# Weight sums in DRAM stored as whole rows of the weights instead of column blocks

## The chip, the cores and the metric

The kernel runs on one core of a Trainium2 chip. The metric is the device time of one execution in microseconds, the median of several runs. The core has TensorE (PE, with its weight loads shown apart as PEld), VectorE (DVE), ScalarE (ACT), GpSimd (POOL) and SyncE (SP). Transfers are issued from SP's queue, from POOL's and a few from ACT's; all of them are moved by the core's 16 DMA engines.

## The reference

One inference step of a two-layer decoder trunk for 1024 prompt tokens and 64 sample tokens, in float32. Layer 0 mixes with a recurrence (12 heads, with low-rank gates) and a memory attention; layer 1 with latent attention. Behind each mixer stands the feed-forward that this change concerns:

```python
def conv_glu(xn, conv_prev, w_up, conv_w, conv_b, w_down):
    T = xn.shape[1]
    u = xn @ w_up                                  # w_up: 1024 x 5632
    gate, val = u[..., :D_FF], u[..., D_FF:]       # D_FF = 2816
    ext = jnp.concatenate([conv_prev.astype(gate.dtype), gate], axis=1)
    conv = conv_b
    for j in range(CONV_W):
        conv = conv + ext[:, j:j + T] * conv_w[j]
    h = jax.nn.silu(conv) * val
    return h @ w_down, ext[:, T:]
```

## The kernel before

The product with `w_up` is computed in seven block products instead of eight, in the manner of Strassen and Winograd. For that, sums of quarters of the weight are needed. The weight of a layer has four quarters of 512 rows and 2816 columns: gate columns and value columns, each with upper and lower rows. `sum_weights` forms four sums per layer in DRAM, by transfers alone: `vg` (upper value plus upper gate), `gg` (upper gate plus lower gate), `vgg` (`vg` plus lower gate) and `all` (`vgg` plus lower value). A sum starts as a copy, made by SP's queue (L1298 from the weights, L1307 from another sum), and is then added to by adding transfers of POOL's queue (L1303, `accum_op=ALU.add`), each of which reads a piece of the weight and the sum and writes the sum. A sum lies in DRAM as 22 blocks of 128 columns, `[22, 128, 4, 128]`: block, row in its group of 128, group, column. A block that the feed-forward loads is thus one contiguous piece, with 2048 bytes for each of 128 partitions.

The feed-forward (`ffn`, `up`) goes through 22 chunks of 128 columns for each of two halves of the tokens. For a chunk `load_up` (L1325) loads seven blocks of 256 KB on SP's queue: three straight from the weight, four from the sums. ACT and DVE split each into a high and a low part (L1327, L1328), and PE multiplies.

The sums are made long before they are read, while the mixer of layer 0 runs (`mixer_a`). The mixer has 12 units: two halves of the tokens by six pairs of heads. In each step `i` of its loop the front of unit `i` (projections with `w_in_a`, loaded at L207, with the low part of the weights made by POOL at L211), the inner part of unit `i-1` and the recurrence of unit `i-2` are woven together, and beside them up to five steps of `sums`, a step being one transfer. The first step of the loop holds the projections of the memory keys and values instead (`memory_kv`, loads at L2188 of `w_mem_kv`). A scheduler then orders the instructions of every engine; each engine and each queue works its list in that order. A transfer that POOL issues stands in POOL's list among the arithmetic, and what is behind it waits.

Lines that are named below: L614 and L615 clear a part of a small weight tile on POOL, L648 is a product with it on PE; L760 masks a tile on POOL, L766 and L913 are copies on ACT behind it, and L909, L917, L924 the chained products of the recurrence on PE; L1060 stores a unit's output.

Of the kernel before, what the change touches and what calls it, by code (L numbers as in the profile page):

```python
# [14 lines left out]
ALU = mybir.AluOpType  # L15
# [9 lines left out]
DFF = 2816  # L25
# [75 lines left out]
class Step:  # L101
# [171 lines left out]
    def mixer_a(s, od, qmd, kvd):  # L273
        nc, tc = s.nc, s.tc
# [50 lines left out]
        def front(u):  # L325
            h, p = u
            if p == 0:
                yield from s.a_norm(h)
                yield from s.a_lora(h)
            if p == 2:  # L330
                yield from s.a_gate(h)
            ctx[u] = {}
            yield from s.a_front(p, h, ctx[u])

        def chain(u):
            h, p = u
            ctx[u]["y"] = s.t(ap, [128, 576], "y", 2)
            for g in s.groups(h):
                yield from s.a_chain(p, h, ctx[u], *g)
            yield from s.a_out(p, h, ctx.pop(u))  # L340
# [29 lines left out]
        sums = s.seq(s.sum_weights(0), s.sum_weights(1))  # L370
        for i in range(nu):
            g = []
            if i == 1:
                for j in range(1, (len(s.prows) + 127) // 128):
                    s.load_params(j, [nc.sync])
            if i > 1:
                g.append((chain(units[i - 2]), s.PW[0] + s.PW[1] * units[i - 2][0], s.PW[2]))
            if i:
                u = units[i - 1]
                g.append((s.a_inner(u[1], u[0], ctx[u]), s.PW[3] + s.PW[4] * u[0], s.PW[5]))  # L380
            g.append((front(units[i]), 130 if units[i][1] else 220))
            if i == 0:
                g.append((mkv, 22))
            else:
                g.append((s.take(sums, 5), 5))
            s.merge(g)
        s.mslot = (ap, "xn", 584, 16)
        s.drain(last(s.seq(s.mem_attention(0, qmd, kvd, od, ("mm", "sm", "sm")), s.memory_kv(kvd, 1, ("sm", "mm", "mm")))))
# [895 lines left out]
    def sum_weights(s, l):  # L1284

        nc, W = s.nc, s.I["w_ffn_up"][l]
        NCH = DFF // 128
        s.wsum[l] = {z: s.t(s.dp, [NCH, 128, 4, 128], f"ws{l}{z}", 1) for z in ("vg", "gg", "vgg", "all")}
        S = s.wsum[l]

        def quarter(f0, k0):
            for k in range(4):
                r = 512 * k0 + 128 * k
                yield k, W[r:r + 128, f0:f0 + DFF].rearrange("p (c f) -> p c f", f=128)

        def put(z, f0, k0):
            for k, w in quarter(f0, k0):
                nc.sync.dma_start(out=S[z][:, :, k].rearrange("c p f -> p c f"), in_=w)  # L1298
                yield

        def add(z, f0, k0):
            for k, w in quarter(f0, k0):
                nc.gpsimd.dma_start(out=S[z][:, :, k].rearrange("c p f -> p c f"), in_=w, accum_op=ALU.add)  # L1303
                yield

        def copy(z, y):
            nc.sync.dma_start(out=S[z].rearrange("c p k f -> p c (k f)"), in_=S[y].rearrange("c p k f -> p c (k f)"))  # L1307
            yield

        yield from s.seq(put("vg", DFF, 0), put("gg", 0, 0), add("vg", 0, 0), add("gg", 0, 1), copy("vgg", "vg"),  # L1310
                         add("vgg", 0, 1), copy("all", "vgg"), add("all", DFF, 1))

    def load_up(s, l, c, first=False):


        nc, W = s.nc, s.I["w_ffn_up"][l]

        def quarter(f0, k0):
            return W[512 * k0:512 * k0 + 512, f0:f0 + 128].rearrange("(k p) f -> p k f", p=128)

        fv, fg = DFF + 128 * c, 128 * c
        S = s.wsum[l]
        for i, src in enumerate((quarter(fv, 0), S["vgg"][c], S["gg"][c], S["vg"][c], quarter(fg, 1), S["all"][c], quarter(fv, 1))):
            w = s.t(s.wp, [128, 4, 128], "wr", 3) if first and i < 3 else s.st([128, 4, 128], "wa", s.WA)
            nc.sync.dma_start(out=w, in_=src)  # L1325
            wh, wl = (s.t(s.up, [128, 4, 128], z, 5, F32R) for z in ("uh", "ul"))
            nc.scalar.copy(wh, w)  # L1327
            nc.vector.tensor_tensor(wl, w, wh.bitcast(F32), ALU.subtract)  # L1328
            yield [(wh[:, k], wl[:, k]) for k in range(4)]

    def ffn(s, l, xs0, after, pre=None):
# [3 lines left out]
        Wd = I["w_ffn_down"][l]  # L1335
        NCH = DFF // 128
        s.lay(([128, 4, 128], "wa", s.WA))

        cprev = s.st([128, NCH, 16], "cprev", 1)
        cout = s.st([128, NCH, 18], "cout", 1)  # L1340
        cs = I["state_conv"][l].rearrange("b j f -> (b j) f")
        q = s.pst("dn")
        for i in range(0, NCH, 4):
            m = min(4, NCH - i)
            stg = s.st([128, 4, 128], "wa", s.WA).rearrange("p a b -> p (a b)")
# [1091 lines left out]
```

## Time and profile before

| | |
|---|---|
| median of 3 runs | 3641.74 us (3635.59 to 3645.61) |
| the profiled execution | 3667.54 us, span 3665.8 us |
| PE, PEld busy | 91%, 78% of the span |
| DVE, ACT, POOL busy | 64%, 47%, 23% |
| mean granted TensorE clock | 0.929 |
| DRAM read, written | 436.67 MB, 118.03 MB |

The page divides the span into 40 slices and shows for each how busy the engines and the DMA engines were and which clock TensorE was granted. "issue" as what ended an idle time means that the engine waited for nothing that the profile shows. Instructions that issue transfers are not counted as busy time of POOL.

### The profile page before, as it was taken

What the parts mean: (1) busy time and instruction counts of PE and PEld (TensorE: products, weight loads), DVE (VectorE), ACT (ScalarE), POOL (GpSimd) and SP (SyncE); (2) the same over time, 40 slices, a digit from 0 to 9 for tenths busy, and PEclk for the clock granted to TensorE, in tenths of its full rate; (3) what the DMA queues carried; (4) which work ended last, traced back from release to release, by engine and by line L of the source; (5) the groups of instructions that cost most, each with busy time, mean ns of one, the idle gap of its engine ahead of it and who ended that gap; (6) DMA issues with size and microseconds to landing.
All of it is one profiled execution on the core that took longest, in us unless ns stands there. A gap on an engine that the chain in (4) does not pass through costs nothing. (4 is left out here: it accounts for less than half of the span.)

```text
span 3665.8 us, 68595 instructions
## 1 busy us (share of the span) xinstructions
PE 3352.4 (91%) x25782; PEld 2855.6 (78%) x25782; DVE 2331.4 (64%) x5353; ACT 1725.2 (47%) x3769; POOL 851.5 (23%) x1204
## 2 busy tenths in 40 slices
PE   6677689999986999999999999989999999999998
PEld 4444457767754899998999888855558999989998
DVE  4454356767654477778777647743444777787776
ACT  4333245544444564455444635533335644455444
POOL 4343332322101231113212500101112311132221
PEclk9876578988898899999999999999999999999999
DMA  8999991111223354455444311235433454445443
GB/s 198 239 218 221 209 203 34 39 42 40 68 60 128 95 158 136 138 147 154 142 133 140 103 53 30 81 118 171 148 112 108 140 147 133 137 134 148 138 137 114
DMA packets 608368, 466.90 MB, mean 127 GB/s; under 512 B 51354, under 2 KB 530350, under 8 KB 603940
## 3 DMA queue, kind: packets, MB, share of 16 engines
q1 hardware_dynamic: 502324, 359.80, 34.4%
q0 software_dynamic: 100768, 98.07, 14.0%
q10 hardware_dynamic: 4944, 4.65, 0.4%
q8 instruction: 202, 3.31, 0.4%
q14 instruction: 130, 1.06, 0.1%
HBM read 436.67 MB, written 118.03 MB: 151 GB/s over the span
## 5 line engine op out<-in xcount | busy, mean ns | idle before, releaser
L1368 PE MATMUL pmm<-xh,uh 128*128 128x272 f32 x2464 | 716.9, 291 | 5.1 <-ACT xh L1137 2.8
L1369 PE MATMUL pmm<-xl,uh 128*128 128x272 f32 x2464 | 713.6, 290 | 3.2 <-DVE xl L1138 2.9
L1370 PE MATMUL pmm<-xh,ul 128*128 128x272 f32 x2464 | 715.3, 291 | 0.4 <-DVE ul L1328 0.4
L1327 ACT CAST uh<-wa 128x512 fp32r<-128x512 f32 x610 | 378.5, 622 | 488.0 <-PE pmm L1369 310.1
L1328 DVE TENSOR_TENSOR ul<-wa,uh 128x512 fp32r<-128x512 f32 x610 | 435.4, 719 | 95.6 <-ACT uh L1327 57.7
L1368 PEld LDWEIGHTS pmm<-xh,uh 128*128 128x128 f32 x2464 | 466.9, 190 | 7.0 <-ACT xh L1137 4.3
L1369 PEld LDWEIGHTS pmm<-xl,uh 128*128 128x128 f32 x2464 | 467.7, 190 | 5.0 <-DVE xl L1138 4.5
L1370 PEld LDWEIGHTS pmm<-xh,ul 128*128 128x128 f32 x2464 | 466.5, 189 | 1.1 <-DVE ul L1328 0.9
L481 PE MATMUL pdn<-hh,wh 128*128 128x272 f32 x1248 | 360.7, 290 | 7.7 <-ACT hh L1137 4.0
L482 PE MATMUL pdn<-hl,wh 128*128 128x272 f32 x1248 | 358.2, 288 | 0.7 <-DVE hl L1138 0.7
L483 PE MATMUL pdn<-hh,wl 128*128 128x272 f32 x1248 | 356.8, 288 | 1.6 <-DVE wl L211 1.6
L210 ACT CAST wh<-wr 128x512 fp32r<-128x512 f32 (+2 forms) x363 | 200.6, 563 | 265.9 <-PE pdn L482 113.0
L1375 POOL TENSOR_TENSOR ext<-nt,nt 128x272 f32<-128x272 f32 (+2 forms) x132 | 118.3, 910 | 881.6 <-ACT uh L1327 714.1
L481 PEld LDWEIGHTS pdn<-hh,wh 128*128 128x128 f32 x1248 | 234.9, 189 | 12.9 <-ACT hh L1137 7.9
L483 PEld LDWEIGHTS pdn<-hh,wl 128*128 128x128 f32 x1248 | 234.6, 189 | 2.5 <-DVE wl L211 2.5
L482 PEld LDWEIGHTS pdn<-hl,wh 128*128 128x128 f32 x1248 | 235.0, 189 | 1.1 <-DVE hl L1138 1.1
L481 PE MATMUL pmm<-xn,wh 128*128 128x292 f32 (+2 forms) x552 | 213.4, 387 | 12.0 <-ACT wh L210 5.3
L1166 DVE TENSOR_TENSOR x<-x,pdn 128x272 f32<-128x272 f32 x288 | 125.3, 435 | 133.7 <-PE pdn L483 133.1
L483 PE MATMUL pmm<-xn,wl 128*128 128x292 f32 (+2 forms) x552 | 206.4, 374 | 2.0 <-POOL wl L211 2.0
L482 PE MATMUL pmm<-xn,wh 128*128 128x292 f32 (+2 forms) x552 | 208.1, 377 | 0.0
L211 DVE TENSOR_TENSOR wl<-wr,wh 128x512 fp32r<-128x512 f32 (+2 forms) x271 | 166.4, 623 | 46.4 <-ACT wh L210 42.5
L211 POOL TENSOR_TENSOR wl<-wr,wh 128x512 fp32r<-128x512 f32 (+1 forms) x92 | 123.6, 1347 | 201.2 <-ACT wh L210 181.8
(760 smaller groups left out, 7963.0 us busy)
## 6 DMA issues: line engine op xcount, KB each, us to landing
wa<-in_w_ffn_up SPq DMA_DIRECT2D x262, 256.0 KB
wr<-in_w_ffn_down SPq DMA_DIRECT2D x164, 256.0 KB
wr<-in_w_in_a SPq DMA_DIRECT2D x84, 256.0 KB
wr<-in_w_o SPq DMA_DIRECT2D x64, 256.0 KB
wa<-ws0vg SPq DMA_DIRECT2D x44, 256.0 KB
wa<-ws0all SPq DMA_DIRECT2D x44, 256.0 KB
wa<-ws1vg SPq DMA_DIRECT2D x44, 256.0 KB
wa<-ws1all SPq DMA_DIRECT2D x44, 256.0 KB
```

Source lines behind the costliest of these rows:

```text
L210: nc.scalar.copy(wh[:, :n, :m], wr[:, :n, :m])
L211: s.wl_eng.tensor_tensor(wl[:, :n, :m], wr[:, :n, :m], wh[:, :n, :m].bitcast(F32), ALU.subtract)
L481: nc.tensor.matmul(ps[:m, :n], wh[:, :m], xh[:, c0:c0 + n], start=(k == 0), stop=False)
L482: nc.tensor.matmul(ps[:m, :n], wh[:, :m], xl[:, c0:c0 + n], start=False, stop=False)
L483: nc.tensor.matmul(ps[:m, :n], wl[:, :m], xh[:, c0:c0 + n], start=False, stop=(k == last))
L1166: nc.vector.tensor_tensor(xv, xv, p[:, :n], ALU.add)
L1327: nc.scalar.copy(wh, w)
L1328: nc.vector.tensor_tensor(wl, w, wh.bitcast(F32), ALU.subtract)
L1368: nc.tensor.matmul(p, wh, xh[:, k], start=k == 0, stop=False)
L1369: nc.tensor.matmul(p, wh, xl[:, k], start=False, stop=False)
L1370: nc.tensor.matmul(p, wl, xh[:, k], start=False, stop=k == 3)
L1375: add = lambda eng, o, a, b, op=ALU.add: eng.tensor_tensor(o, a, b, op)
```

## The change

Each sum lies in DRAM as the quarter itself does, `[512, 2816]`. Every copy and every adding transfer moves 128 whole rows. A copy from the weights moves rows of 11264 bytes. A copy from another sum is cut into four transfers of 128 rows, which the compiler lays out as 32 pieces of 45056 bytes, where there was one transfer for the whole sum before. An adding transfer is limited to pieces of 5632 bytes, so that it has 128 by 2 of them, where it had 128 by 22 pieces of 512 bytes. Steps per layer become 32 instead of 26, and the mixer takes up to six of them per unit. `load_up` now picks its block out of the rows, so that all seven loads of a chunk read pieces of 512 bytes.

```diff
-                g.append((s.take(sums, 5), 5))
+                g.append((s.take(sums, 6), 6))
...
-        s.wsum[l] = {z: s.t(s.dp, [NCH, 128, 4, 128], f"ws{l}{z}", 1) for z in ("vg", "gg", "vgg", "all")}
-        S = s.wsum[l]
...
-        def put(z, f0, k0):
-            for k, w in quarter(f0, k0):
-                nc.sync.dma_start(out=S[z][:, :, k].rearrange("c p f -> p c f"), in_=w)
-                yield
-
-        def add(z, f0, k0):
-            for k, w in quarter(f0, k0):
-                nc.gpsimd.dma_start(out=S[z][:, :, k].rearrange("c p f -> p c f"), in_=w, accum_op=ALU.add)
-                yield
-
-        def copy(z, y):
-            nc.sync.dma_start(out=S[z].rearrange("c p k f -> p c (k f)"), in_=S[y].rearrange("c p k f -> p c (k f)"))
-            yield
-
-        yield from s.seq(put("vg", DFF, 0), put("gg", 0, 0), add("vg", 0, 0), add("gg", 0, 1), copy("vgg", "vg"),
-                         add("vgg", 0, 1), copy("all", "vgg"), add("all", DFF, 1))
+        S = s.wsum[l] = {z: s.t(s.dp, [512, DFF], f"ws{l}{z}", 1) for z in ("vg", "gg", "vgg", "all")}
+
+        def move(z, src, **kw):
+            eng = nc.gpsimd if kw else nc.sync
+            for r in range(0, 512, 128):
+                eng.dma_start(out=S[z][r:r + 128], in_=src[r:r + 128], **kw)
+                yield
+
+        def add(z, src):
+            return move(z, src, accum_op=ALU.add, max_dma_last_dim=5632)
+
+        g1, g2, v1, v2 = (W[r:r + 512, f:f + DFF] for f in (0, DFF) for r in (0, 512))
+        yield from s.seq(move("vg", v1), move("gg", g1), add("vg", g1), add("gg", g2), move("vgg", S["vg"]),
+                         add("vgg", g2), move("all", S["vgg"]), add("all", v2))
...
-        for i, src in enumerate((quarter(fv, 0), S["vgg"][c], S["gg"][c], S["vg"][c], quarter(fg, 1), S["all"][c], quarter(fv, 1))):
+        for i, (src, r, f) in enumerate(((W, 0, fv), (S["vgg"], 0, fg), (S["gg"], 0, fg), (S["vg"], 0, fg), (W, 512, fg), (S["all"], 0, fg), (W, 512, fv))):
...
-            nc.sync.dma_start(out=w, in_=src)
+            nc.sync.dma_start(out=w, in_=src[r:r + 512, f:f + 128].rearrange("(k p) f -> p k f", p=128))
```

The scheduler orders the mixer's instructions anew on every engine. On POOL, in the middle of the units of the first half of the tokens, where the sum `gg` of layer 1 (`ws1gg`) gets its additions, this stood before (the last number is the shape; for a transfer it is partitions by pieces by numbers in a piece):

```order
L1303 DMA ws1gg_4343<-in_w_ffn_up 128x22x128
L494 MEMSET ext_3295 128x1
L1303 DMA ws1gg_4343<-in_w_ffn_up 128x22x128
L614 MEMSET wl_3254 64x128
L615 MEMSET wl_3254 64x128
L1303 DMA ws1gg_4343<-in_w_ffn_up 128x22x128
L499 COPY carry_163<-ext_2731 128x1
L710 TENSOR_SCALAR bv_2835<-bv_2835,ptile_20_120 128x512
L760 TENSOR_TENSOR t_615_2809<-q_2807,c_tmask_138 64x256
```

and this stands there now:

```order
L1292 DMA ws1gg_4472<-in_w_ffn_up 128x2x1408
L760 TENSOR_TENSOR t_615_2812<-q_2810,c_tmask_138 64x256
L614 MEMSET wl_3258 64x128
L615 MEMSET wl_3258 64x128
L211 TENSOR_TENSOR wl_3289<-wr_3286,wh_3288 128x512
L1292 DMA ws1vgg_4473<-in_w_ffn_up 128x2x1408 x2
L710 TENSOR_SCALAR bv_2839<-bv_2839,ptile_20_120 128x512
L760 TENSOR_TENSOR t_615_2812<-q_2811,c_tmask_138 64x256
```

Of the three additions that stood around the two clearings and ahead of the mask, one is left there, and the next two, of the next sum, stand behind them in one run; there are 32 additions in all, as before.

On SP's queue, where the sum `vgg` of layer 0 starts as a copy of `vg`, this stood before:

```order
L2203 DMA out_mem_v_p<-q_702 128x256
L1307 DMA ws0vgg_753<-ws0vg_751 128x22x512
L207 DMA wr_1514<-in_w_in_a 128x4x128
L207 DMA wr_1520<-in_w_in_a 128x4x128
L624 DMA wr_1911<-in_w_g_up 128x128
```

and this stands there now:

```order
L2189 DMA out_mem_v_p<-q_702 128x256
L207 DMA wr_1459<-in_w_in_a 128x4x128
L207 DMA wr_1465<-in_w_in_a 128x4x128
L207 DMA wr_1515<-in_w_in_a 128x4x128
L1292 DMA ws0vgg_753<-ws0vg_751 32x11264 x2
L207 DMA wr_1521<-in_w_in_a 128x4x128
L1292 DMA ws0vgg_753<-ws0vg_751 32x11264
L624 DMA wr_1913<-in_w_g_up 128x128
```

The one copy of the whole sum has become four (the first of them stands a few rows earlier, ahead of the stores of the memory keys), and loads of the mixer's weights stand between them.

## Rows read from the trace of the kernel before

**Rows 1.** The span in 40 equal slices: busy tenths of PE and of the DMA engines.
```profile
PE   6677689999986999999999999989999999999998
...
DMA  8999991111223354455444311235433454445443
```

**Rows 2.** Busy time by stretch: length, then engines; clock, DMA share, GB/s last.
```profile
40.00:540.00 500.00, 355.43 (x2516) 232.59 (x2514) 240.43 (x655) 176.06 (x396) 182.67 (x188) 0.73 1.22 221
540.00:1040.00 500.00, 474.86 (x4431) 347.61 (x4430) 336.68 (x1057) 245.17 (x606) 129.68 (x208) 0.88 0.19 48
```

**Rows 3.** Line L1303, the adding transfers: POOL's idle us before them, times.
```profile
  issue: 118.1, 16
  DMA ws0gg<-in_w_ffn_up: 34.2, 4
  DMA ws0vg<-in_w_ffn_up: 13.0, 1
```

**Rows 4.** POOL in order of time, 370 to 420: start, duration, instruction, [idle before].
```profile
396.92 2.44 POOL L1303 DMA_DIRECT2D ws1gg<-in_w_ffn_up  x1 [20.55 <-issue]
399.40 0.20 POOL L614 MEMSET wl<- 64x128 f32 x1
...
410.81 2.46 POOL L1303 DMA_DIRECT2D ws1gg<-in_w_ffn_up  x1 [10.97 <-issue]
```

**Rows 5.** ACT in order of time, 385 to 420.
```profile
415.74 0.40 ACT L766 COPY q<-kr 64x256 f32<-64x256 f32 x1 [14.99 <-POOL t L760]
```

**Rows 6.** PE in order of time, 385 to 420.
```profile
399.65 0.58 PE L648 MATMUL psm<-lw_st,wl 128*128 128x260 f32 x1 [11.08 <-POOL wl L614]
...
416.30 0.48 PE L917 MATMUL pch<-r,XT 64*64 64x64 f32 x4 [14.19 <-ACT r L913]
```

**Rows 7.** Waits of PE, 40 to 540: total us, times, longest.
```profile
PE pch L2193 <- ACT q L1137: 37.2, 7, 12.1
PE pch L917 <- ACT r L913: 29.5, 4, 14.2
PE pch L909 <- DVE s L935: 13.4, 4, 11.7
PE psm L648 <- POOL wl L614: 11.1, 1, 11.1
```

**Rows 8.** Waits of all engines, 40 to 540: two that end with a load.
```profile
ACT q L1137 <- DMA q<-in_w_mem_kv: 46.1, 7, 13.8
...
ACT wh L210 <- DMA wr<-in_w_in_a: 40.8, 12, 13.5
```

**Rows 9.** SP's queue in order of time, 45 to 110.
```profile
58.43 12.03 SPq L2188 DMA_DIRECT2D q<-in_w_mem_kv  x1
```

**Rows 10.** All DMA packets, 40 to 540: packets, MB, rate, sizes.
```profile
DMA packets 175768, 110.34 MB, mean 221 GB/s; under 512 B 6096, under 2 KB 161384, under 8 KB 175736
```

**Rows 11.** DMA queues, 420 to 430: packets, MB, share (q0 POOL's, q1 SP's).
```profile
q0 software_dynamic: 3545, 1.81, 143.9%
```

**Rows 12.** DMA queues, 240 to 260.
```profile
q0 software_dynamic: 3971, 2.03, 79.1%
q1 hardware_dynamic: 3970, 2.00, 50.5%
```

**Rows 13.** DMA queues, 475 to 485.
```profile
q1 hardware_dynamic: 1529, 3.13, 103.1%
```

**Rows 14.** DMA queues, 271 to 286.
```profile
q1 hardware_dynamic: 1738, 3.56, 71.0%
q0 software_dynamic: 1741, 0.88, 46.1%
```

**Rows 15.** Line L207, 0 to 540: issues of the loads of w_in_a, ns min, median, longest.
```profile
L207 SPq DMA_DIRECT2D wr<-in_w_in_a x54: 367/506/16936, 16.0 to 526.4; - x54
```

**Rows 16.** Busy time in most of the first feed-forward, columns as in rows 2.
```profile
1300.00:2000.00 700.00, 686.07 (x5371) 680.10 (x5370) 532.74 (x960) 354.72 (x640) 153.13 (x247) 0.99 0.50 145
```

**Rows 17.** DMA queues in the first feed-forward, 1400 to 1900.
```profile
q1 hardware_dynamic: 95975, 71.45, 49.2%
```

More of the change, by code (lines that the diff above doesn't have):

```diff
@@ L1286, in sum_weights @@
         nc, W = s.nc, s.I["w_ffn_up"][l]
-        NCH = DFF // 128
-        s.wsum[l] = {z: s.t(s.dp, [NCH, 128, 4, 128], f"ws{l}{z}", 1) for z in ("vg", "gg", "vgg", "all")}
-        S = s.wsum[l]
[L1291 to L1294, printed above, removed]
-        def put(z, f0, k0):
-            for k, w in quarter(f0, k0):
-                nc.sync.dma_start(out=S[z][:, :, k].rearrange("c p f -> p c f"), in_=w)
-                yield
@@ L1313, in load_up @@
     def load_up(s, l, c, first=False):
         nc, W = s.nc, s.I["w_ffn_up"][l]
-        def quarter(f0, k0):
-            return W[512 * k0:512 * k0 + 512, f0:f0 + 128].rearrange("(k p) f -> p k f", p=128)
         fv, fg = DFF + 128 * c, 128 * c
         S = s.wsum[l]
-        for i, src in enumerate((quarter(fv, 0), S["vgg"][c], S["gg"][c], S["vg"][c], quarter(fg, 1), S["all"][c], quarter(fv, 1))):
+        for i, (src, r, f) in enumerate(((W, 0, fv), (S["vgg"], 0, fg), (S["gg"], 0, fg), (S["vg"], 0, fg), (W, 512, fg), (S["all"], 0, fg), (W, 512, fv))):
```

## The prediction

> **What bounds the kernel now.** I read the slices of the page first, to see in which stage transfers matter. The DMA engines are busy 9 tenths in the first six slices, up to about 540 us, and near 1 or 2 tenths in the next; PE stands at 6 to 8 tenths in those six slices and at 9 in almost every later one [rows 1]. The busy times of two stretches put numbers on it: from 40 to 540 us PE is busy 355.4 us of 500 at a granted clock of 0.73, from 540 to 1040 it is busy 474.9 us at 0.88 [rows 2]. Both stretches are the mixer of layer 0; what the first has and the second has not is the making of the sums. So the question is what 144.6 us of idle PE and a low clock in the first stretch hang on.
>
> Next the line of the adding transfers: POOL sat idle 118.1 us before 16 of them with no releaser that shows, and 47.2 us before 5 that waited for the copy they add to [rows 3]. One piece of time shows what that does to PE. POOL waits 20.55 us before one addition, and only then clears a weight tile; PE's L648 waits for this tile, 11.08 us. POOL waits 10.97 us before the next addition; ACT's L766 waits 14.99 us for the mask behind it, and PE's L917 waits 14.19 us for ACT [rows 4 to 6]. In the first stretch as a whole PE waits 37.2 us in the memory keys (L2193), 29.5 us at L917, 13.4 us at L909 and 11.1 us at L648 [rows 7]. The 37.2 us end with loads: ACT waits 46.1 us for blocks of `w_mem_kv` [rows 8], and SP itself took 12.03 us to issue one [rows 9], with 2816 pieces of a sum put in its queue ahead.
>
> **What a piece costs.** From 420 to 430 us POOL's queue ran nearly alone: 3545 packets in 10 us on 16 engines, 45.1 ns for an addition of 512 bytes [rows 11]. From 240 to 260 us both queues ran: 320 us of engine time less 3971 times 45.1 ns leaves 35.5 ns for each of SP's 3970 packets of 512 bytes [rows 12]. From 475 to 485 us a copy of 2048-byte pieces ran alone: 1529 packets, 104.6 ns each, 313 GB/s [rows 13]. Through the two copies goes a line of 12.5 ns a packet and 0.045 ns a byte.
>
> The account of before: 16 copies from the weights with 2816 packets at 35.5 ns are 100 us on 16 engines; 4 whole copies, 11264 packets at 104.6 ns, are 74 us; 32 additions, 90112 packets at 45.1 ns, are 254 us. That is 428 us for 92.3 MB. The other 18.0 MB of the stretch's 110.3 MB [rows 10] at 512 bytes in 35.5 ns are 78 us. Together 506 us for a stretch of 500: the DMA engines were full, and POOL moved at their pace.
>
> After: each of the 32 copies is 1.44 MB. A row of 11264 bytes costs 519 ns by the line, eight rows an engine 4.15 us, 133 us in all; if long pieces are no faster than the row of 2048 bytes, 147 us. Pieces of 45056 bytes cost the same per byte within 3%. An addition of 5632 bytes does not occur in the trace. A copy of that size costs 266 ns by the line; an addition of 512 bytes costs 9.6 ns more than a copy. If that is paid once a packet, 276 ns, 16 an engine, 141 us for all 32; if an addition gains nothing from length, 11 times 45.1 = 496 ns and 254 us. I take 9.6 ns for every 512 bytes, 372 ns and 190 us, since both of its parts come from rows. The sum is 323 us (274 to 401) where it was 428: 105 us less (27 to 154).
>
> A rule of the Trainium skill speaks against any of this: the page DMA: Bandwidth & Descriptors, section Specifications, puts the smallest transfer at line rate at 512 bytes, so by it the old pieces were already as fast as longer ones, and the sum would be nil. The trace does not agree, with 202 GB/s at 512 bytes and 313 at 2048 [rows 12, 13].
>
> **The sum on the path.** Five terms.
> First, the loads of `w_mem_kv`. A put ahead of them takes 4.15 us instead of 6.2 alone and some 14 with additions alternating (176 packets an engine at 35.5 ns, or at 35.5 and 45.1). I take two thirds of the 37.2 us off: -25 us.
> Second, POOL. With 256 pieces instead of 2816 the wait without a releaser should go: I read it as a queue that is full, since the two additions shown stand 13.9 us apart [rows 4], about what one takes with as many copy packets between: 176 packets an engine at 45.1 and 35.5 ns, 14.2 us. The PE waits at L917, L909 and L648 go with it: -54 us [rows 7].
> Third, the clock. With 79 us less idle, PE is busy 84% of the stretch; between 71% at 0.73 and 95% at 0.88 [rows 2] that lies at 0.81. 355.4 us at 0.73 are 319 us at 0.81: -36 us.
> Fourth, what comes in its place: an addition still waits for the copy of its own rows, and in POOL's list all the mixer's low weight parts and masks stand behind it, for which PE waits. Before, such waits were 47.2 us [rows 3]; a copy now takes 4.15 us instead of 14: +14 us. Copies of sums on SP wait for additions likewise, with loads of the mixer behind them; there are 16 instead of 4, each a quarter, and I put that at nothing, because the loads stand three weight tiles ahead of PE.
> Fifth, the feed-forwards. Four of seven loads go from 2048 to 512 bytes a piece. Of 95975 packets of 745 bytes on average [rows 17], 14.5 thousand are of 2048; they become 58 thousand, 129 us of engine time instead of 95 in 500 us, so the share goes from 0.49 to 0.56. PE is 98% busy there [rows 16] and hides it; without that cover it would be 34 us in 500, 95 us over 1400 us. Only the first loads of each feed-forward stand open, eight of them, 0.84 us before and 1.14 after: +2 us.
>
> Sum: -25 -54 -36 +14 +2 = -99 us. The DMA engines allow it: they shed 105 us. The profiled execution would go from 3667.5 to 3568 us; the median lies 25.8 us below it, so I predict **3543 us**.
>
> **The rivals.**
> *More than the named waits goes.* If the first stretch ran as densely as the second (95% at 0.88), its work of 355.4 times 0.73 would take 310 us: 190 us less, 3452 us. For it: DVE and ACT also shed waits. Against it: the chained products of the recurrence (L909, L917, L924) set a pace of their own.
> *The additions gain nothing from length.* Then the DMA time falls by 27 us at most and stays the pace: 3615 to 3642 us. For it: no row shows an addition over 512 bytes. Against it: 9.6 ns over a copy is little for a second operand that would have to be paid in full.
> *Length gains nothing at all*, because 512 bytes is already the best rate: 3642 us, no change. Rows 12 and 13 speak against it. It is the rule of the Trainium skill's page named above.
> *Loads wait behind long pieces: slower.* While both queues ran, 1738 packets of one went beside 1741 of the other, though these were four times as long [rows 14]: the engines alternate packet by packet. A load of 256 KB has 32 packets an engine; beside it went as many additions of 45.1 ns, 1.4 us. Now up to 16 of 372 to 496 ns go first, 6 to 8 us. Of some 62 loads (54 of `w_in_a` [rows 15] and 8 of `w_mem_kv`) half would meet an addition; 31 times 6 us is 186 us if all of it stands open, against terms of -115: 71 us slower, 3713 us. It decides from 3.7 us exposed a load. Against it: loads are issued ahead, and ACT waited only 40.8 us in all for `w_in_a` [rows 8] with the queues full. The Trainium skill, same page, section Queues, rings and completion order, says that an engine goes round its queues packet by packet; rows 14 agree.
>
> **How the numbers follow.** The forecast has 0.65, its own range 3492 to 3602 (gains of 150 to 40 us, the ends of the DMA account with some of the 27 used up). The denser stretch has 0.12, additions without gain 0.11, no gain from length 0.03, slower 0.09. The range of 3455 to 3630 leaves out 0.02 of the second, 0.05 of the third and the last two, 0.19. About 0.3% (11 us) is what a measurement can tell from no change. Faster: 0.65 + 0.12 + 0.06 of the additions without gain = 0.83. Same: 0.05 + 0.03 + 0.01 = 0.09. Slower: 0.08.
>
> **What would show it.** In the profile after, the idle time without a releaser before the additions should be under 20 us; packets of POOL's queue in the sums some 270 to 500 ns long; PE's waits at L2193, L917 and L648 mostly gone; the six full DMA slices with gaps or fewer of them; the clock between 40 and 440 us at 0.8 or more; the feed-forwards as long as now with a DMA share near 0.56. The prediction is wrong if POOL's waits without a releaser stay (the queue is full for another reason), if the waits for `w_in_a` on ACT grow past 100 us, or if a feed-forward grows by more than 5 us.

## The result, and the profile after

The changed kernel takes **3604.49 us** (median of 5 runs, 3599.70 to 3614.81). The kernel before took 3641.74 us in runs beside it (5 runs, 3635.59 to 3651.04). The ratio is 0.990 with a 95% interval of 0.9875 to 0.9925, a gain of 37 us where 98 were forecast. Measured again later, the ratio was 0.9868 (0.9832 to 0.9903). The sign is right and the time lies in the range, but six tenths of the gain are missing. The profiled execution is the one of 3604.49 us, its span 3602.7 us; that of before was 25.8 us above its median, so the two traces lie 63 us apart and the medians 37.

The slices of the page after, to be held against [rows 1] (PE, the granted clock in tenths, and the DMA engines):

```profile
PE   6678789999996999999999899999999999999998
...
PEclk9877769999887999999999999999999999999999
...
DMA  7999931111314354445444310335424544545443
```

The DMA engines are full in slices 2 to 5; the sixth went from 9 to 3. So the transfers end earlier, but while they last the engines are as full as they were, and the clock is at 0.7 and 0.6 in slices 3 to 6. (The DMA share adds up the times of packets. Before, packets overlapped on an engine and it came to 1.22 in the first stretch [rows 2]; so the kernels are compared by bytes and packets, not by this share.) Busy time by stretch (length, then PE, PEld, DVE, ACT, POOL; clock, DMA share, GB/s), the first two and the last against [rows 2, 16]:

```profile
40.00:540.00 500.00, 380.67 (x2737) 245.39 (x2736) 257.07 (x750) 195.15 (x448) 142.72 (x196) 0.74 0.86 225
540.00:1040.00 500.00, 474.57 (x4695) 346.95 (x4693) 341.13 (x1076) 248.74 (x625) 126.59 (x207) 0.93 0.19 50
200.00:300.00 100.00, 80.42 (x751) 50.58 (x752) 51.66 (x153) 37.93 (x92) 30.25 (x44) 0.70 0.96 256
300.00:400.00 100.00, 72.94 (x560) 45.00 (x559) 45.78 (x151) 34.72 (x83) 24.55 (x34) 0.71 0.99 256
1300.00:2000.00 700.00, 691.18 (x5444) 685.81 (x5443) 542.18 (x983) 356.36 (x654) 157.46 (x254) 1.00 0.49 140
```

PE is idle for 119.3 us of the first stretch instead of 144.6, 25 less where 79 were forecast, and its clock there is 0.74 instead of 0.73. In the second stretch PE is busy as long as before, 474.57 and 474.86 us, but the clock is 0.93 instead of 0.88. The feed-forward's DMA share stayed at 0.49.

The line of the sums' transfers, L1292 now (issues: count, ns min, median, longest, first and last start; then POOL's idle us before them, and times), against [rows 3]:

```profile
L1292 POOL DMA_DIRECT2D ws1all<-in_w_ffn_up x4: 1145/1153/1211, 411.4 to 463.3; - x4
...
  DMA ws0gg<-in_w_ffn_up: 15.1, 4
...
  issue: 0.5, 2
```

The wait without a releaser is gone, 118.1 us to 0.5, and an issue of an addition costs POOL 1.15 us instead of 2.46. The last addition is issued at 463 us; before it was 529. But the waits of all engines from 40 to 540 us (total us, times, longest), against [rows 7, 8], have changed their names rather than gone:

```profile
POOL wl L211 <- ACT wh L210: 123.8, 22, 14.2
ACT wh L210 <- DMA wr<-in_w_in_a: 89.5, 13, 13.3
...
PE py L949 <- ACT q L918: 26.5, 9, 12.0
PE pch L2179 <- ACT q L1137: 25.9, 5, 10.7
ACT q L1137 <- DMA q<-in_w_mem_kv: 22.3, 4, 10.4
...
PE pmm L481 <- ACT wh L210: 17.5, 4, 9.6
...
PE pch L917 <- ACT r L913: 13.4, 3, 9.4
```

ACT's wait for blocks of `w_in_a` went from 40.8 to 89.5 us. PE waits less at L917 (13.4 instead of 29.5) and in the memory keys (25.9 instead of 37.2, now L2179), but 26.5 us at L949 and 17.5 us at L481, which had 7.8 and 5.3. One piece of time shows the link. SP issues two loads at 297.78 us:

```profile
297.78 1.00 SPq L207 DMA_DIRECT2D wr<-in_w_in_a  x2
```

Meanwhile the two queues go packet for packet, as in [rows 14], but POOL's packets are long ones now (305 to 310 us):

```profile
q0 software_dynamic: 168, 0.94, 91.9%
q1 hardware_dynamic: 167, 0.20, 13.8%
```

At this pace the 512 pieces of a load take 15 us; from 305 to 315 us in the kernel before, with 1968 of SP's packets beside 1962 of POOL's in 10 us, they took 2.6. ACT in order of time waits 12.71 us for a load:

```profile
320.13 0.62 ACT L210 CAST wh<-wr 128x512 fp32r<-128x512 f32 x1 [12.71 <-DMA wr<-in_w_in_a]
```

and PE stands for nearly the same time behind ACT's next piece of work:

```profile
320.91 0.47 PE L949 MATMUL py<-q,q 128*64 128x64 f32 x2 [11.95 <-ACT q L918]
```

What the copies and what the additions gained, the two DMA queues show from 200 to 300 us (packets, MB, share; q0 POOL's, q1 SP's). Before:

```profile
q0 software_dynamic: 18855, 9.60, 75.5%
q1 hardware_dynamic: 16485, 12.58, 52.1%
```

After:

```profile
q0 software_dynamic: 1834, 9.70, 50.6%
q1 hardware_dynamic: 6694, 15.79, 44.9%
```

In a tenth of the packets POOL's queue moved 9.70 MB in 100 us where it had moved 9.60: in this window the additions run no faster. SP's queue moved 15.79 instead of 12.58 MB. In the windows beside it POOL's queue did move more, 11.39 MB instead of 7.78 from 100 to 200 us and 11.09 instead of 9.26 from 300 to 400. Whether that comes from the additions' own pieces or from the new copies beside them, these rows can't tell; the experiment with pieces of 512 bytes does.

Where the 63 us between the traces lie: the mixer of layer 0 ends with the store of its last unit at L1060. In the trace of before:

```profile
1146.50 0.33 SPq L1060 DMA_DIRECT2D odp<-y  x1
```

In the trace after:

```profile
1095.52 0.33 SPq L1060 DMA_DIRECT2D odp<-y  x1
```

That is 51 us. The first feed-forward, from its copy of `cprev` to its last store of `xd`, takes 760.3 us in both traces. Some 12 us lie in layer 1's mixer, where the change has nothing; the 25.8 us by which the traced execution of before lies above its median may account for that, which is not shown.

### The profile page after: what moved, and what is told of

Read it like the earlier page. It is cut to its first block, busy times and chain, and to the rows that moved or that the text cites. A ratio compares the mean times of both kernels' runs of the same rounds, so it can differ in the third digit from the quotient of the medians.

```text
span 3602.7 us, 68623 instructions
## 1 busy us (share of the span) xinstructions
PE 3329.3 (92%) x25782; PEld 2838.5 (79%) x25782; DVE 2322.9 (64%) x5353; ACT 1722.7 (48%) x3769; POOL 806.1 (22%) x1204
## 5 line engine op out<-in xcount | busy, mean ns | idle before, releaser
L481 PE MATMUL pdn<-hh,wh 128*128 128x272 f32 x1248 | 360.9, 290 | 7.7 <-ACT hh L1137 3.9
L483 PE MATMUL pdn<-hh,wl 128*128 128x272 f32 x1248 | 357.2, 288 | 1.6 <-DVE wl L211 1.6
L481 PEld LDWEIGHTS pdn<-hh,wh 128*128 128x128 f32 x1248 | 235.3, 189 | 12.9 <-ACT hh L1137 7.9
L483 PEld LDWEIGHTS pdn<-hh,wl 128*128 128x128 f32 x1248 | 235.0, 189 | 2.5 <-DVE wl L211 2.5
L481 PE MATMUL pmm<-xn,wh 128*128 128x292 f32 (+2 forms) x552 | 214.6, 389 | 21.3 <-ACT wh L210 17.5
L483 PE MATMUL pmm<-xn,wl 128*128 128x292 f32 (+2 forms) x552 | 204.2, 371 | 1.6 <-POOL wl L211 1.4
```

The lines of the kernel that those rows point to most:

```text
L481: nc.tensor.matmul(ps[:m, :n], wh[:, :m], xh[:, c0:c0 + n], start=(k == 0), stop=False)
L483: nc.tensor.matmul(ps[:m, :n], wl[:, :m], xh[:, c0:c0 + n], start=False, stop=(k == last))
```

## The experiments

The theory after the result: the mixer's first half is paced by the DMA engines' time for the additions, whatever POOL waits for, and an addition gains little from longer pieces. The rivals: POOL's place in line; the length of the pieces ahead of the mixer's loads; the copies. In the three kernels that change only the additions (pieces of 512 bytes, of 2816 bytes, plain copies) every engine works the same list of instructions in the same order as in the changed kernel, by their traces (at most 7 of PE's 25782 rows stand otherwise); so the order is no rival there.

**What the sums cost in all.** Two kernels, each from the changed one: without the additions, and without any sum.

```diff
-        yield from s.seq(move("vg", v1), move("gg", g1), add("vg", g1), add("gg", g2), move("vgg", S["vg"]),
-                         add("vgg", g2), move("all", S["vgg"]), add("all", v2))
+        yield from s.seq(move("vg", v1), move("gg", g1), move("vgg", S["vg"]), move("all", S["vgg"]))
```

> The changed kernel without its 32 adding transfers (the sums stay plain copies, so this part of the result is left out). Theory: the DMA engines still set the pace of the mixer's first half in the changed kernel, since an addition of 5632 bytes costs some 420 ns and the 32 of them some 215 us; without them the DMA account of the stretch falls from some 430 to some 215 us and the time to 3490 to 3530 us, ACT's waits for w_in_a from 89.5 to under 30 us. Rival 1, the loads wait behind the long pieces of the additions: the same direction, the waits for w_in_a nearly gone. Rival 2, the mixer's own chains set the pace now: 3590 to 3605 us.

Measured 3475.60 us, 0.9525 of the kernel before (0.9487 to 0.9563). Its first stretch:

```profile
40.00:540.00 500.00, 462.42 (x4044) 321.00 (x4043) 351.88 (x1019) 266.25 (x611) 153.13 (x222) 0.90 0.44 143
```

Its copies show the price of long pieces. From 171 to 176 us nearly all bytes are in pieces of 11264:

```profile
DMA packets 138, 1.37 MB, mean 275 GB/s; under 512 B 16, under 2 KB 16, under 8 KB 16
q1 hardware_dynamic: 138, 1.37, 95.4%
```

From 127 to 131 us they are in pieces of 45056:

```profile
DMA packets 51, 1.58 MB, mean 394 GB/s; under 512 B 16, under 2 KB 16, under 8 KB 16
```

The first is 288 GB/s at a full share. The kernel without any sum:

```diff
-        sums = s.seq(s.sum_weights(0), s.sum_weights(1))
+        sums = iter(())
...
-        for i, (src, r, f) in enumerate(((W, 0, fv), (S["vgg"], 0, fg), (S["gg"], 0, fg), (S["vg"], 0, fg), (W, 512, fg), (S["all"], 0, fg), (W, 512, fv))):
+        for i, (src, r, f) in enumerate(((W, 0, fv), (W, 0, fg), (W, 0, fg), (W, 0, fg), (W, 512, fg), (W, 0, fg), (W, 512, fv))):
```

> The changed kernel without any making of sums; all seven loads of a chunk read blocks of the weight itself in pieces of 512 bytes (the sums are left out of the result). It bounds what the sums cost in all. Theory: 3460 to 3500 us, the first 500 us of the mixer at a clock and PE share like those of the second half. Rival 2, the chains of the mixer set the pace: 3570 to 3600 us. If it lies within 15 us of the kernel without additions, the copies cost nothing.

Measured 3475.16 us, 0.9526 (0.9485 to 0.9566). The two are equal: with no additions beside them, the copies with long pieces cost nothing that can be measured. The sums cost 176 us before (3651.57 less 3475.16, in runs side by side) and some 129 after (3604.49 less 3475.16, from runs at two times; 3.4 to 3.7% by the ratios), and after the change all of it goes with the additions. For the short copies of before no run shows this. Without the additions PE is 92% busy in the first stretch at a clock of 0.90, and ACT waits 0.3 us for `w_in_a`.

**The additions in pieces of 512 bytes again**, everything else as changed. This brings POOL's full queue back.

```diff
-            return move(z, src, accum_op=ALU.add, max_dma_last_dim=5632)
+            return move(z, src, accum_op=ALU.add, max_dma_last_dim=512)
```

> The changed kernel with the adding transfers cut into pieces of 512 bytes again, in rows of 2816 numbers; copies and loads as in the change. Theory (the additions' DMA time and POOL's full queue are what the change saved): 3620 to 3645 us, POOL's idle time without a releaser before additions back at 80 us or more. Rival 1 (what the change lost is loads that wait behind long pieces): faster than the changed kernel's 3604, at 3570 to 3595 us, and ACT's waits for w_in_a back at some 40 us.

Measured 3626.43 us, 0.9934 (0.9909 to 0.996). The time lies in the theory's range, but the kernel before took 3651.57 us in the runs beside it, so that most of the gain is still there. POOL's idle time before the additions is back, and more of it than before the change:

```profile
  issue: 188.2, 23
```

yet ACT's wait for `w_in_a` is 31.1 us instead of 89.5. PE waits for POOL instead, 23.6 us at L483 for low weight parts (0.8 with long pieces), and is busy 383.26 us in the first stretch, as after (380.67). The queues from 200 to 300 us move what they move after:

```profile
q0 software_dynamic: 18835, 9.59, 77.0%
q1 hardware_dynamic: 6556, 15.72, 47.6%
```

From 100 to 400 us POOL's queue moved 32.53 MB with short pieces and 32.18 with long ones. Beside the same copies the length of the pieces makes no difference to the additions' pace in these 300 us.

The same kernel was run a second time beside the changed one, on one chip.

> The changed kernel once more, beside the next one on the same chip: a ratio near 0.990 to the kernel before.

> The changed kernel with additions in pieces of 512 bytes once more, to size what POOL's full queue is worth by itself. By the prediction's second term (54 us for POOL's waits): a ratio of 1.003 to 1.006 to the kernel before. By the waits that moved to the loads instead: 0.992 to 0.995, some 10 to 15 us over the changed kernel.

Measured 3605.01 us, 0.9868 (0.9832 to 0.9903), for the changed kernel, and 3612.15 us, 0.988 (0.9846 to 0.9914), for the short pieces. The latter is below both expectations. In the two pairs the long pieces of the additions are worth 0.34% (runs at two times) and 0.12% (side by side; 0.2% by the medians), some 12 and 4 us, and the intervals overlap in both; the change as a whole is worth 1.0% and 1.3%. So most of the gain must come from the rest of the change, presumably from the longer copies: from 100 to 400 us POOL's queue moved 32.53 MB beside them, and 26.63 beside the short copies of the kernel before, in pieces of 512 bytes both times. A kernel with short copies and long additions, which would show it, was not run. A wait of 142 to 188 us on POOL is worth little by itself here.

**Half the piece.** If loads wait behind long pieces, shorter ones must help.

```diff
-            return move(z, src, accum_op=ALU.add, max_dma_last_dim=5632)
+            return move(z, src, accum_op=ALU.add, max_dma_last_dim=2816)
```

> The changed kernel with additions in pieces of 2816 bytes. Theory (DMA time): from 45 ns at 512 bytes and 420 ns at 5632 a line gives 214 ns, so 219 us for all instead of 215, POOL's queue not full: within 8 us of the changed kernel, 3600 to 3615 us. Rival 1 (loads wait behind long pieces): the pieces are half as long, so 3570 to 3590 us, and ACT's waits for w_in_a near 50 us instead of 89.5.

Measured 3592.90 us, 0.9892 (0.9863 to 0.9921): no difference from the change by the ratio. ACT waits 88.3 us for `w_in_a`, as with 5632 bytes. The queues still go packet for packet, now twice as fast (305 to 310 us):

```profile
q0 software_dynamic: 336, 0.90, 93.4%
q1 hardware_dynamic: 333, 0.17, 16.7%
```

So a load's 512 pieces pass in 7.7 us instead of 15, and yet the sum of the waits is the same: between 2816 and 5632 bytes the length of the piece ahead of a load does not set it.

**The additions as plain copies**, of the same pieces in the same queue and order.

```diff
-            return move(z, src, accum_op=ALU.add, max_dma_last_dim=5632)
+            return move(z, src, max_dma_last_dim=5632)
```

> The changed kernel with its 32 adding transfers turned into plain copies on the same queue, with the same pieces of 5632 bytes (the additions are left out of the result). The additions cost some 130 us, as the runs without them show; is it the adding or the long pieces beside the loads? Theory (the adding reads two operands, so that its DMA time is some 215 us where a copy takes some 135): 3520 to 3560 us. Rival 1 (any piece of 5632 bytes on the other queue holds the loads up): 3590 to 3605 us.

Measured 3518.68 us, 0.9671 (0.9634 to 0.9708), 2.2 points under the kernel with 2816-byte additions, which ran beside it. Its queues from 200 to 300 us:

```profile
q1 hardware_dynamic: 6160, 16.94, 52.6%
q0 software_dynamic: 2577, 13.70, 39.6%
```

A plain packet of 5632 bytes takes 39.6% of 1600 us by 2577, 246 ns; an adding one after the change 50.6% of 1600 by 1834, 441 ns. ACT's wait for `w_in_a` falls to 15.6 us. An adding packet of 2816 bytes held an engine as long as a plain one does here (59.8% of 1600 us by 4091 packets, 234 ns), with 88.3 us of waits; but there were 16384 of those, and here there are 8192. So, where POOL's queue is not full, the wait of the loads goes with the total time that POOL's transfers hold the engines and not with the length of one packet. The plain copies are not free either: 0.9671 is 1.5 points above the kernel without additions (0.9525, measured at another time).

**Less of it at a time.** If the engines' share is the pace, it should help to take the sums slowly. A first attempt gave half the steps to each unit of the mixer and layer 1's sums to the feed-forward of layer 0.

```diff
-        sums = s.seq(s.sum_weights(0), s.sum_weights(1))
+        sums = s.sum_weights(0)
...
-                g.append((s.take(sums, 6), 6))
+                g.append((s.take(sums, 3), 3))
...
+        sums = s.sum_weights(1) if l == 0 else iter(())
...
-                s.merge([(down(*order[n - 1]), 16), (s.take(u, 64), 64)])
+                s.merge([(down(*order[n - 1]), 16), (s.take(u, 64), 64), (s.take(sums, 4), 4)])
```

> The changed kernel with the sums of layer 1 made during the feed-forward of layer 0 instead of in the mixer, so that the mixer holds half the transfers. Theory: the DMA engines stop being the pace of the mixer: 3530 to 3560 us, the feed-forward unchanged within 5 us, with a DMA share of some 0.65. Rival 2, the mixer's chains set the pace: 3595 to 3605 us. A third case, the transfers disturb the feed-forward: that stage longer by over 10 us.

Measured 3603.37 us, 0.986 (0.9821 to 0.9899). It tests nothing: the scheduler drew the transfers forward into the mixer, and the DMA slices of the mixer's first half are those of the changed kernel, but for the sixth, which is at 2 instead of 3. So the next kernel only pins the sums to the place at which the program emits them.

```diff
-                eng.dma_start(out=S[z][r:r + 128], in_=src[r:r + 128], **kw)
+                s.tc.keep_in_program_order(eng.dma_start(out=S[z][r:r + 128], in_=src[r:r + 128], **kw))
```

> The changed kernel with the sums' transfers held in the order in which the program emits them on their queues, so that they spread over all units of the mixer, some 1000 us, instead of the first 450. Theory (the transfers matter because they come so densely that the DMA engines are full): 3510 to 3560 us, DMA share under 0.6 in each stretch of 100 us. Rival 1 (a load beside an addition waits, wherever that is): the same number of loads meets additions, 3590 to 3605 us.

Measured 3543.61 us, 0.9745 (0.9711 to 0.978). The last addition is now issued at 838 us instead of 463, and the first stretch is

```profile
40.00:540.00 500.00, 442.67 (x3586) 309.31 (x3585) 329.68 (x948) 248.39 (x566) 167.42 (x227) 0.85 0.64 170
```

with 13.5 us of waits for `w_in_a`. The share was expected under 0.6 in each 100 us; it is 0.76 from 100 to 200 us and 0.49 to 0.69 in the stretches from there to 800. From 135 to 140 us the additions run alone, which gives the price that no row of before had:

```profile
q0 software_dynamic: 168, 0.95, 96.5%
```

96.5% of 80 us by 168 is 459 ns for 5632 bytes, 196 GB/s. The window holds the start of a transfer; from 136 to 141 us 188 packets pass in 80 us of engine time, 426 ns, 212 GB/s. So the price is 426 to 459 ns.

The pin and the split together:

> The same, with the sums of layer 1 held in the feed-forward of layer 0 (the earlier attempt at that did not move them: the scheduler drew them forward into the mixer). Theory: half the transfers in the mixer, over all its units: 3490 to 3530 us, the feed-forward of layer 0 within 5 us. A further case: the additions disturb the feed-forward, its length grows by over 10 us.

Measured 3522.89 us, 0.9689 (0.9662 to 0.9716), the fastest kernel here that computes everything. Its DMA slices show no full stretch in the mixer, and the rest of the work in the feed-forward:

```profile
DMA  5444343342142768869673210344423544545443
```

That is not free: the feed-forward (first start of `cprev` to last of `xd`)

```profile
L1335 ACT COPY cprev<-pdn x2: 452/452/452, 1173.2 to 2755.8; 128x352 f32<-128x352 f32 x2
```

```profile
L1573 SPq DMA_DIRECT2D xd<-x x4: 366/412/762, 1569.7 to 1952.0; - x4
```

takes 778.8 us, 18.5 more, where at most 5 were expected, while the mixer's last store starts at 991.4 us, 104 earlier than after the change.

**The old layout, spread alike**: the kernel before, with its additions of 512 bytes, the same pin on its three kinds of transfer and the same split.

```diff
-                nc.gpsimd.dma_start(out=S[z][:, :, k].rearrange("c p f -> p c f"), in_=w, accum_op=ALU.add)
+                s.tc.keep_in_program_order(nc.gpsimd.dma_start(out=S[z][:, :, k].rearrange("c p f -> p c f"), in_=w, accum_op=ALU.add))
```

> The kernel before, its column blocks and 512-byte additions untouched, with its sums spread as in the last run: layer 0's over the mixer's units, layer 1's in the feed-forward of layer 0, both in program order. It tells whether the layout is worth anything once the transfers do not come densely. Theory (what matters is how full the DMA engines are while the mixer runs; the longer pieces save some 90 us of DMA time in all, most of it then hidden): 3530 to 3560 us, within 1% of the spread kernel with whole rows. Rival (short pieces cost by POOL's full queue wherever they stand): 3580 to 3640 us.

Measured 3549.04 us, 0.9716 (0.9665 to 0.9766). Beside 0.9689 for the new layout, measured at another time, the intervals overlap: once the sums are spread, the layout is worth 0.3% by these two, and anything from nothing to 0.8% fits. The traces lean to the new one: the mixer's last store starts at 1005.2 us instead of 991.4, and the feed-forward takes 794.5 us, 34.2 more than without sums in it, where the new layout took 18.5 more.

## Why the prediction was right in sign and wrong in size

The start held. In the first half of layer 0's mixer the DMA engines are full, the sums fill them, and PE's idle time and low clock hang on that: without sums the kernel is 176 us faster than before. The steps:

- **The price of an addition failed, and with it the size of the gain.** The prediction took 372 ns for 5632 bytes, on the ground that a second operand paid in full would cost more than the 9.6 ns seen at 512 bytes. It is paid nearly in full: 426 to 459 ns alone, 1.7 to 1.9 times the 246 ns of a plain piece, between the 372 taken and the upper bound of 496. All 32 additions, 8192 packets on 16 engines, are then 218 to 235 us, where 190 were forecast and 254 stood before. With the copies at 288 to 394 GB/s in the kernel without additions, 46.1 MB are 117 to 160 us. The account falls from 428 to between 335 and 395 us, by 33 to 93 instead of 105. In the mixed stretch even the additions' 19 to 36 us don't show (32.53 and 32.18 MB from 100 to 400 us beside the same copies). The rival "the additions gain nothing from length" had this mechanism, with 0.11 and 3615 to 3642 us; the result is 10 us below it.
- **The second term, POOL's queue (-54 us), failed as a step of the sum.** Its reading was right: with 256 pieces the wait without a releaser fell to 0.5 us, and with 512-byte pieces it came back. But it was a symptom. The additions had to pass through the same engines in nearly the same time, and what POOL no longer waited for, ACT waited for as loads of `w_in_a`. With the queue full again the kernel lost 4 to 12 us, which is not clear of the noise.
- **The third term, the clock (-36 us)**, followed the second: 0.74, not 0.81, since PE's idle time fell by 25 us, not 79. Other first stretches have 0.80 at 443.50 us busy (plain copies), 0.85 at 442.67 (pinned) and 0.90 at 462.42 (no additions). The first two have the same busy time and different clocks, so the line that the prediction drew through two stretches does not give the clock. What it had not counted is the second stretch, 0.93 instead of 0.88. By busy time times clock PE did 22 us more of work at full clock in the first stretch of this pair of traces (380.67 at 0.74 against 355.43 at 0.73) and 24 us more in the second: an estimate by which half of the gain lies behind the sums.
- **The first term, the loads of `w_mem_kv`**, had the right sign: -11 us at L2179 instead of -25.
- **The fourth term was too small.** POOL's wait for copies is 15.1 us before `ws0gg` and some 22 in all, where 14 were forecast. (The sum counted the 14 as a loss, though such waits stood at 47.2 before.) But loads of the mixer held up by the sums were put at nothing, since they stand three weight tiles ahead, and ACT's wait for `w_in_a` grew by 48.7 us. The rival with long pieces names the right place, and its alternation is there, 168 packets beside 167. It does not explain the size: half-length pieces leave the wait as it is, and plain copies of the same length nearly end it.
- **The fifth term, the feed-forward (+2 us)**: 760.3 us in both traces. The share did not rise to 0.56 (0.49), so by the share 512-byte loads into the core's memory cost no more engine time than 2048-byte ones; the cover was not needed.

The rule of the Trainium skill that the prediction set against the trace (page DMA: Bandwidth & Descriptors, section Specifications: line rate from 512 bytes on) comes out in two halves. For copies in DRAM the trace does not agree: 231 GB/s at 512 bytes by the 35.5 ns of [rows 12], 313 at 2048 [rows 13], 288 to 394 at 11264 and more. (The 202 GB/s that the prediction gives for 512 bytes is both queues together, half of it additions.) For additions alone it comes nearer: 182 GB/s at 512 bytes [rows 11], 196 to 212 at 5632. The prediction let the copies' rows speak for the additions. The same page, section Issuing engines are not separate DMA queues, says that all transfers run on the same 16 engines and interleave, whichever engine issued them; the trace agrees, since with POOL's queue no longer full its transfers moved no more data beside the same copies (32.18 MB against 32.53).

What stays open: how much of the 37 us is the additions' (the two pairs say 4 to 12 us); how the rest divides between the copies and the new order of the mixer's instructions, which no run separates; by what path the additions' total time, and not the length of one piece, holds the loads up; and the 12 us between the traces in layer 1's mixer.

## What to carry to other kernels

When the DMA engines are full for a whole stretch, add up engine time and treat the waits in it as one: a wait removed on one engine returns on another unless engine time goes. Price an adding transfer by its own row, not from a copy's: here an addition of 5632 bytes cost 1.7 to 1.9 copies. And ask first whether bulk transfers must run in the stretch that is short of engines: spreading these gave 2.8% in the old layout, the new layout 1.0 to 1.3% by itself and about 0.3% on top, which the intervals do not tell from nothing; look at the slices to see that the scheduler left them where they were put.

## What the runs showed that was not expected

- An addition of 5632 bytes takes 426 to 459 ns alone, a plain copy of as much 246 ns beside other transfers; at 512 bytes the two were 45.1 and 35.5 ns [rows 11, 12].
- The time that POOL takes to issue an addition depends on its pieces: 2.46 us with 2816 of them, 1.15 us with 256.
- The mixer's loads wait alike beside additions of 5632 and 2816 bytes (ACT 89.5 and 88.3 us), though a load passes twice as fast beside the shorter ones. They wait less at 512 bytes (31.1 us), where POOL's own queue was full; that the full queue spared the loads is not shown by itself.
- In the feed-forward, where the DMA share was 0.49 without them, 16 additions and their copies still cost 18.5 us, and 34.2 in the old layout.
